# Input units of the first half written whole: fifteen high products, sixteen low products, the closing high one

## The chip, the cores and the metric

One core of a Trainium2 chip runs the whole program. The metric is the device time of one execution in microseconds (us); the time before is the median of three runs. TensorE (PE) multiplies, ScalarE (ACT) and VectorE (DVE) work on tiles in SBUF and PSUM, GpSimd is POOL, and SyncE (SP) issues nearly all loads of weights.

## The reference

One layer of a hybrid encoder trunk on x of 256 tokens by 2048 features, in float32:

```python
u = rms_norm(x); proj = u @ w_in            # 2048 x 12,580 columns
y_a = stick_breaking_attention(...)         # 4 heads x 128
y_b = forgetting_attention(...)             # 4 heads x 128
y_c = rwkv7_time_mix(...)                   # 16 heads x 64, a recurrence over 256 tokens
m = sum_i sigmoid(gate_i) * (y_i @ P_i)
x = x + rms_norm(m @ w_out)
x = x + rms_norm(relu(rms_norm(x) @ w_up)**2 @ w_down)
```

What matters here is `proj`: a product of the transposed input (2048 rows, that is sixteen blocks of 128) with blocks of 128 columns of `w_in`.

## The kernel before

**Split products.** Every matrix is used as the sum of two float32r parts. The input `u` is split into sixteen tiles `pk`, each of 128 x 512: the high part of the 256 tokens in the left half, the low part in the right half. A weight half tile of 128 x 1024 (eight blocks of 128 x 128, 512 KB) is loaded by SP into a buffer `raw`; ACT copies it to `whi`, the high part (L158), and DVE subtracts that from `raw` into `wlo`, the low part (L159). A *high product* multiplies a block of `whi` with all 512 columns of a `pk` tile, a *low product* a block of `wlo` with the left 256 columns alone. Sixteen of each make one *input unit*, a PSUM tile `gps` of 128 x 512, whose two halves are added when it is read.

**Units.** `unit` makes one input unit out of two half tiles. `gemm` writes eight high and eight low products of a half tile; in the second half the last high product comes last of all (L182), since it writes all 512 columns and closes the sum. Lines: L174 high, L178 low, L182 closing. `unit` is called 39 times, all in the first 320 us: for five of the eight query and key tiles of the stick-breaking attention (h = 3 to 7, at 24 to 54 us; the first three are written by hand), for eight of the forgetting attention, two low-rank ones and 24 of the RWKV branch. The other users of `gemm`, the up-projection of the MLP, do not go through `unit`. Between groups of units `tok` makes token-major products, in which each product, high or low, has 512 columns (L204, L220).

**Buffers and order.** `raw`, `whi` and `wlo` have three buffers each, in turn. `wnext` hands out the next split half tile and sees that one more is already asked for (`AHEAD = 1`). A `wlo` buffer comes free when its last low product is done, a `raw` buffer when its `wlo` has been written; SP issues loads in order, so a load waits for the DVE split that frees its buffer. PE runs in the order in which the program writes its instructions. ACT and DVE are put in order by a scheduler when the program is built, and then run strictly in that order.

**Beside the units.** The attention and RWKV steps are generators. `tick`, called after every two high or four low products, moves a clock and lets the generators write their next instructions between the products. At h = 4 `norm` works out 1/rms of the tokens (`rstd`: ACT L247 and L248, DVE L249 to L252); `scaled` (L403) multiplies the finished tiles by it. At h = 7 `narrow_weights` (L418) builds a small weight tile out of two further `raw` loads.

Of the kernel before, what the change touches and what calls it, by code (L numbers as in the profile page):

```python
# [17 lines left out]
T = 256  # L18
D = 2048
KT = 16  # L20
AHEAD = 1
SETTLE = 2.6
US = 0.227
# [27 lines left out]
def hybrid_block(ctx, tc, xt, x, gains, params, consts, lora, gup, wst, out):  # L51
    nc = tc.nc
    V, A, G, PE = nc.vector, nc.scalar, nc.gpsimd, nc.tensor
# [15 lines left out]
    def gps():  # L69
        return pg.tile([128, 512], F32, tag="gps", name=nm("gps"), bufs=4)  # L70
# [35 lines left out]
    def step(th):  # L106

        if th["need"] is not None:
            if th["need"] not in at or clock[0] < at[th["need"]] + SETTLE:
                return False  # L110
            th["need"] = None
        if clock[0] < th["due"]:
            return False
        try:
            r = next(th["gen"])
        except StopIteration:
            threads.remove(th)
            return True
        if isinstance(r, str):
            th["need"] = r  # L120
        else:
            th["due"] = clock[0] + r
        return True

    def tick(us):

        clock[0] += us
        while any([step(th) for th in list(threads)]):
            pass
# [13 lines left out]
    def wraw(n=None):  # L143
        raw = wpool.tile([128, HALF], F32, tag="raw", name=nm("raw"), bufs=3)
        nc.sync.dma_start(out=raw, in_=wst[wpos[0] if n is None else n])
        wpos[0] = (wpos[0] if n is None else n) + 1
        return raw
# [3 lines left out]
    def wsplit(raw):  # L151
        home = homes.pop(0) if homes else None
        if home:
            hi, lo = home(), home()
        else:
            hi = wpool.tile([128, HALF], F32R, tag="whi", name=nm("whi"), bufs=3)
            lo = wpool.tile([128, HALF], F32R, tag="wlo", name=nm("wlo"), bufs=3)
        A.activation(hi, raw, AF.Copy)  # L158
        V.tensor_tensor(lo, raw, hi.bitcast(F32), ALU.subtract)  # L159
        wq.append((hi, lo))  # L160

    def wnext():

        while len(wq) < 1 + AHEAD and (order or wpos[0] < wst.shape[0]):
            wsplit(wraw(order.pop(0) if order else None))
            if side:
                side.pop(0)()
        return wq.pop(0)

    def gemm(ps, hi, lo, pks, first, last, tick=lambda us: None):  # L170

        n = len(pks)
        for i in range(n - 1 if last else n):
            PE.matmul(ps, hi[:, i * 128:i * 128 + 128], pks[i], start=first and i == 0, stop=False)  # L174
            if i % 2:
                tick(2 * US)
        for i in range(n):
            PE.matmul(ps[:, 0:T], lo[:, i * 128:i * 128 + 128], pks[i][:, 0:T], start=False, stop=False)  # L178
            if i % 4 == 3:
                tick(2 * US)  # L180
        if last:
            PE.matmul(ps, hi[:, (n - 1) * 128:n * 128], pks[n - 1], start=False, stop=True)  # L182

    def unit(pks):

        ps = gps()
        for h in range(2):
            hi, lo = wnext()
            gemm(ps, hi, lo, pks[8 * h:8 * h + 8], h == 0, h == 1, tick)
        return ps  # L190

    def tok(pks, lag=1):
# [253 lines left out]
    for h in range(8):  # L446
        if h == 7:
            wz = narrow_weights()
        ps = qb[h] if h < 3 else unit(upk)
        qk.append(g1())  # L450
        evac(ps, qk[h])
        if h == 4:
            ms = norm()
        if h == 6:
            turned_rstd(ms)
        for i in range(h + 1) if h == 4 else [h] if h > 4 else []:
            scaled(qk[i])
# [621 lines left out]
    def low_rank(i):  # L1079
        nme, n = (("zx", 128), ("zy", 128))[i]  # L1080
        ps = unit(upk)
        z = rp.tile([128, T], F32, tag=nme, name=nme, bufs=1)
        shift(ps, MU_X + i, z[0:n], n)
        done[nme] = z
# [3 lines left out]
    for s in ("q", "k"):  # L1088
        lst = []
        for h in range(4):  # L1090
            ps = unit(upk)
            t = g1()
            evac(ps, t)
            scaled(t)
            lst.append(t)
        done["fox" + s] = lst
# [7 lines left out]
    for hf in range(2):  # L1104
        for s, mo in (("k", MU_K), ("r", MU_R), ("v", MU_V)):
            for p in range(4 * hf, 4 * hf + 4):
                ps = unit(upk)
# [213 lines left out]
    work, urgent, tasks, hl = [], [], [], {}  # L1321
# [237 lines left out]
    for j in range(2):  # L1559
        up(j)  # L1560
        ps, post = heads[j]
# [241 lines left out]
```

## Time and profile before

| | us |
|---|---|
| median of three runs | 1492.98 (1491.58 to 1494.12) |
| the profiled execution's own time | 1491.24 |
| its span, first to last instruction | 1489.5 |
| PE busy | 1476.4 (99%) |
| DVE busy | 1214.5 (82%) |
| ACT busy | 933.4 (63%) |
| granted clock of PE, mean | 0.998 |

The table gives each engine's busy time within the span. PE's is nearly the span; the other engines work beside it. Names such as `whi<-raw` say which tile is written from which.

### The profile page before, as it was taken

What the parts mean: (1) busy time and instruction counts of PE and PEld (TensorE: products, weight loads), DVE (VectorE), ACT (ScalarE), POOL (GpSimd) and SP (SyncE); (2) the same over time, 40 slices, a digit from 0 to 9 for tenths busy, and PEclk for the clock granted to TensorE, in tenths of its full rate; (3) what the DMA queues carried; (4) which work ended last, traced back from release to release, by engine and by line L of the source; (5) the groups of instructions that cost most, each with busy time, mean ns of one, the idle gap of its engine ahead of it and who ended that gap; (6) DMA issues with size and microseconds to landing.
All of it is one profiled execution on the core that took longest, in us unless ns stands there. A gap on an engine that the chain in (4) does not pass through costs nothing.

```text
span 1489.5 us, 22848 instructions
## 1 busy us (share of the span) xinstructions
PE 1476.4 (99%) x8427; PEld 1248.4 (84%) x8427; DVE 1214.5 (82%) x1688; ACT 933.4 (63%) x1394; POOL 90.0 (6%) x160
## 2 busy tenths in 40 slices
PE   9999999999999999999999999999999999999997
PEld 8888888888778888788888888888888888888885
DVE  7676778999678898567647788999899999999986
ACT  7465666654576554474444777776767767777653
POOL 0011000100001100000000000000000000000000
PEclk9999999999999999999999999999999999999999
DMA  7545454545544546445855768888888887989874
GB/s 285 189 164 183 161 177 169 184 159 198 174 148 167 183 164 208 142 158 189 272 193 207 273 209 254 255 257 255 247 255 251 267 256 223 260 249 283 259 249 155
DMA packets 107759, 317.70 MB, mean 213 GB/s; under 512 B 10752, under 2 KB 14976, under 8 KB 107392
## 3 DMA queue, kind: packets, MB, share of 16 engines
q1 hardware_dynamic: 94688, 284.39, 55.4%
q0 software_dynamic: 8064, 29.36, 10.6%
q10 hardware_dynamic: 4896, 2.49, 0.6%
q8 instruction: 66, 1.08, 0.3%
q14 instruction: 45, 0.37, 0.1%
HBM read 282.65 MB, written 4.19 MB: 193 GB/s over the span
## 4 chain that ended last, share of the span: by engine, by line
PE 98%; DVE 1%; DMA 0%; issue 0%; ACT 0%; POOLq 0%; POOL 0%; DVEq 0%; ACTq 0%
PE gps L220 28%; PE gps L174 23%; PE gps L178 13%; PE gps L204 7%; PE mps L1511 3%; PE mps L1512 3%; PE mps L1513 3%; PE gps L1511 3%; PE gps L1513 3%; PE gps L1512 3%; PE gps L182 2%; PE gps L340 1%; PE mps L828 1%; PE gps L1270 0%; PE gps L338 0%; DMA x<-in_xt_dram 0%
## 5 line engine op out<-in xcount | busy, mean ns | idle before, releaser
L159 DVE TENSOR_TENSOR wlo<-raw,whi 128x1024 fp32r<-128x1024 f32 x495 | 600.9, 1221 | 154.2 <-ACT whi L158 139.4
L158 ACT ACTIVATE whi<-raw 128x1024 fp32r<-128x1024 f32 x495 | 521.5, 1057 | 253.9 <-PE gps L220 87.4
L174 PE MATMUL gps<-pk,whi 128*128 128x512 f32 x1321 | 332.4, 392 | 0.0
L220 PE MATMUL gps<-whi,pk 128*128 128x512 f32 x1136 | 286.4, 392 | 0.0
L174 PEld LDWEIGHTS gps<-pk,whi 128*128 128x128 f32 x1321 | 244.7, 188 | 47.6
L220 PEld LDWEIGHTS gps<-whi,pk 128*128 128x128 f32 x1136 | 211.4, 188 | 44.1 <-issue 0.4
L178 PEld LDWEIGHTS gps<-pk,wlo 128*128 128x128 f32 x1408 | 192.0, 190 | 13.6
L178 PE MATMUL gps<-pk,wlo 128*128 128x256 f32 x1408 | 196.9, 283 | 0.0
L220 PE MATMUL gps<-wlo,pk 128*128 128x512 f32 x568 | 155.3, 392 | 0.0
L220 PEld LDWEIGHTS gps<-wlo,pk 128*128 128x128 f32 x568 | 105.7, 188 | 22.0
L1374 DVE TENSOR_TENSOR sp<-raw,sp 128x1024 fp32r<-128x1024 f32 x67 | 81.7, 1220 | 3.4 <-ACT sp L1373 3.1
L1402 ACT ACTIVATE sp<-gps 128x512 f32<-128x512 f32 x52 | 31.1, 598 | 84.3 <-PE gps L182 84.3
L1373 ACT ACTIVATE sp<-raw 128x1024 fp32r<-128x1024 f32 x67 | 70.7, 1055 | 14.1 <-PE mps L1512 5.1
L204 PE MATMUL gps<-whi,pk 128*128 128x512 f32 x256 | 68.9, 390 | 0.0
L1511 PE MATMUL mps<-whi,fm 128*128 128x512 f32 x168 | 66.2, 394 | 0.0
L1512 PE MATMUL mps<-whi,fm 128*128 128x512 f32 x168 | 65.8, 392 | 0.0
L1513 PE MATMUL mps<-wlo,fm 128*128 128x512 f32 x168 | 65.6, 390 | 0.0
L1473 POOL DMA_DIRECT2D raw<-raw x40 | 35.0, 874 | 427.4 <-DVE raw L1470 108.4
L204 PEld LDWEIGHTS gps<-whi,pk 128*128 128x128 f32 x256 | 47.8, 188 | 9.9
L1511 PE MATMUL gps<-whi,fm 128*128 128x512 f32 x126 | 49.3, 391 | 0.0
L1513 PE MATMUL gps<-wlo,fm 128*128 128x512 f32 x126 | 49.1, 390 | 0.0
L1470 DVE TENSOR_TENSOR raw<-raw,raw 128x1024 f32<-128x1024 f32 x40 | 48.8, 1220 | 0.4
(400 smaller groups left out, 2013.4 us busy)
## 6 DMA issues: line engine op xcount, KB each, us to landing
raw<-in_wst_dram SPq DMA_DIRECT2D x499, 512.0 KB, 4.4
raw<-raw POOLq DMA_DIRECT2D x40, 512.0 KB, 6.4
sp<-in_wst_dram SPq DMA_DIRECT2D x16, 512.0 KB, 5.3
raw<-sp POOLq DMA_DIRECT2D x8, 512.0 KB, 6.2
sp<-raw POOLq DMA_DIRECT2D x8, 512.0 KB, 6.4
x<-in_x_dram SPq DMA_DIRECT2D x8, 256.0 KB, 5.5
xs<-x SPq DMA_DIRECT2D x2, 1024.0 KB, 4.8
x<-xs SPq DMA_DIRECT2D x4, 512.0 KB, 6.5
```

Of the source, the lines that this page charges most:

```text
L158: A.activation(hi, raw, AF.Copy)
L159: V.tensor_tensor(lo, raw, hi.bitcast(F32), ALU.subtract)
L174: PE.matmul(ps, hi[:, i * 128:i * 128 + 128], pks[i], start=first and i == 0, stop=False)
L178: PE.matmul(ps[:, 0:T], lo[:, i * 128:i * 128 + 128], pks[i][:, 0:T], start=False, stop=False)
L204: PE.matmul(ps[tt], pks[k][:, c:c + 128], w[:, (k - k0) * 512:(k - k0) * 512 + 512], start=k == 0 and part == 0 and w is hl[0], stop=w is ...
L220: PE.matmul(ps[tt], pks[k][:, c:c + 128], w[:, (k - k0) * 512:(k - k0) * 512 + 512], start=k == 0 and part == 0 and w is hl[0], stop=False)
L1373: A.activation(hi, raw, AF.Copy)
L1374: V.tensor_tensor(lo, raw, hi.bitcast(F32), ALU.subtract)
L1470: V.tensor_tensor(x, x, z, ALU.add)
L1511: PE.matmul(Q[f], p, w, start=d == 0 and i == 0, stop=False)
L1512: PE.matmul(Q[f], pl, w, start=False, stop=False)
L1513: PE.matmul(Q[f], p, wl, start=False, stop=d == nd - 1 and i == 1)
```

## The change

`unit` no longer calls `gemm`. It writes fifteen high products through both half tiles, then sixteen low products through both, then the sixteenth high product. The second `wnext` now stands between the eighth and the ninth high product. The calls of `tick` are as many as before (eleven in a unit), seven among the high and four among the low products.

```diff
     def unit(pks):
 
         ps = gps()
-        for h in range(2):
-            hi, lo = wnext()
-            gemm(ps, hi, lo, pks[8 * h:8 * h + 8], h == 0, h == 1, tick)
+        hl = []
+
+        def high(k):
+            PE.matmul(ps, hl[k // 8][0][:, k % 8 * 128:k % 8 * 128 + 128], pks[k], start=k == 0, stop=k == KT - 1)
+
+        for k in range(KT - 1):
+            if k % 8 == 0:
+                hl.append(wnext())
+            high(k)
+            if k % 2:
+                tick(2 * US)
+        for k in range(KT):
+            PE.matmul(ps[:, 0:T], hl[k // 8][1][:, k % 8 * 128:k % 8 * 128 + 128], pks[k][:, 0:T], start=False, stop=False)
+            if k % 4 == 3:
+                tick(2 * US)
+        high(KT - 1)
         return ps
```

Lines below the change stand 13 further down in the changed kernel (L249 becomes L262, L403 L416); high products are now L190, low ones L199. Numbers at the end of names are running numbers and differ a little between the programs: `whi_539` of before is `whi_531` now.

PE, the middle of the unit h = 7, before: the end of the first half's high products, its low products, and the start of the second half's.

```order
L174 MATMUL gps_577<-pk_190,whi_539 128x512
L174 MATMUL gps_577<-pk_193,whi_539 128x512
L178 MATMUL gps_577<-pk_132,wlo_540 128x256
L178 MATMUL gps_577<-pk_135,wlo_540 128x256
L178 MATMUL gps_577<-pk_144,wlo_540 128x256
L178 MATMUL gps_577<-pk_147,wlo_540 128x256
L178 MATMUL gps_577<-pk_180,wlo_540 128x256
L178 MATMUL gps_577<-pk_183,wlo_540 128x256
L178 MATMUL gps_577<-pk_190,wlo_540 128x256
L178 MATMUL gps_577<-pk_193,wlo_540 128x256
L174 MATMUL gps_577<-pk_222,whi_580 128x512
L174 MATMUL gps_577<-pk_225,whi_580 128x512
```

The same place now:

```order
L190 MATMUL gps_577<-pk_190,whi_531 128x512
L190 MATMUL gps_577<-pk_193,whi_531 128x512
L190 MATMUL gps_577<-pk_222,whi_580 128x512
L190 MATMUL gps_577<-pk_225,whi_580 128x512
L190 MATMUL gps_577<-pk_228,whi_580 128x512
L190 MATMUL gps_577<-pk_231,whi_580 128x512
L190 MATMUL gps_577<-pk_244,whi_580 128x512
L190 MATMUL gps_577<-pk_247,whi_580 128x512
L190 MATMUL gps_577<-pk_250,whi_580 128x512
L199 MATMUL gps_577<-pk_132,wlo_532 128x256
L199 MATMUL gps_577<-pk_135,wlo_532 128x256
L199 MATMUL gps_577<-pk_144,wlo_532 128x256
```

The first use of `whi_580`, the second half's high part, moved forward past the eight low products of the first half.

DVE, at the end of h = 5, before: splits of weights (L159) and the steps of 1/rms (L249 to L252).

```order
L159 TENSOR_TENSOR wlo_490<-raw_487,whi_489 128x1024
L159 TENSOR_TENSOR wlo_518<-raw_515,whi_517 128x1024
L249 TENSOR_TENSOR tmp_451<-rstd_312 128x256
L250 TENSOR_TENSOR tmp_451<-tmp_451,tmp_450 128x256
L251 TENSOR_SCALAR tmp_451<-tmp_451 128x256
L252 TENSOR_TENSOR rstd_312<-rstd_312,tmp_451 128x256
L234 TENSOR_TENSOR g_76_509<-gps_464,tmp_510 128x256
L403 TENSOR_TENSOR g_45_343<-g_45_343,rstd_312 128x256
```

The same place now:

```order
L159 TENSOR_TENSOR wlo_482<-raw_479,whi_481 128x1024
L262 TENSOR_TENSOR tmp_451<-rstd_312 128x256
L263 TENSOR_TENSOR tmp_451<-tmp_451,tmp_450 128x256
L159 TENSOR_TENSOR wlo_518<-raw_515,whi_517 128x1024
L264 TENSOR_SCALAR tmp_451<-tmp_451 128x256
L265 TENSOR_TENSOR rstd_312<-rstd_312,tmp_451 128x256
L247 TENSOR_TENSOR g_76_509<-gps_464,tmp_510 128x256
L416 TENSOR_TENSOR g_45_343<-g_45_343,rstd_312 128x256
```

The split `wlo_518` (second half of h = 6) moved back past two steps of 1/rms. In both programs five more rows of `scaled` follow, then the split of the first half of h = 7 (`wlo_540`, now `wlo_532`) and the two rows of `narrow_weights`.

## Rows read from the trace of the kernel before

**Rows 1.** The page: span and busy time by engine.
```profile
span 1489.5 us, 22848 instructions
...
PE 1476.4 (99%) x8427; PEld 1248.4 (84%) x8427; DVE 1214.5 (82%) x1688; ACT 933.4 (63%) x1394; POOL 90.0 (6%) x160
```

**Rows 2.** Waits of PE, whole span: total us, times, longest.
```profile
PE mps L281 <- DVE zt L278: 1.2, 1, 1.2
PE gps L340 <- DVE pk L243: 0.9, 1, 0.9
PE mps L1255 <- DVE x L1217: 0.5, 1, 0.5
PE mps L962 <- DVE XT L949: 0.3, 1, 0.3
```

**Rows 3.** Timeline of PE, one unit: start, us, line, operation, shape, count.
```profile
104.58 2.00 PE L174 MATMUL gps<-pk,whi 128*128 128x512 f32 x8
106.41 1.11 PE L178 MATMUL gps<-pk,wlo 128*128 128x256 f32 x8
107.36 1.78 PE L174 MATMUL gps<-pk,whi 128*128 128x512 f32 x7
108.97 1.12 PE L178 MATMUL gps<-pk,wlo 128*128 128x256 f32 x8
...
110.16 2.00 PE L174 MATMUL gps<-pk,whi 128*128 128x512 f32 x8
```

**Rows 4.** Timeline of PE in a stretch of 512-column products alone.
```profile
68.76 1.97 PE L220 MATMUL gps<-whi,pk 128*128 128x512 f32 x8
...
71.48 1.98 PE L220 MATMUL gps<-whi,pk 128*128 128x512 f32 x8
```

**Rows 5.** Timeline of PE, the unit h = 7.
```profile
48.32 2.12 PE L174 MATMUL gps<-pk,whi 128*128 128x512 f32 x8
50.28 1.11 PE L178 MATMUL gps<-pk,wlo 128*128 128x256 f32 x8
51.23 1.78 PE L174 MATMUL gps<-pk,whi 128*128 128x512 f32 x7
```

**Rows 6.** Timeline of ACT, 36 to 52 us: two of its rows.
```profile
41.19 0.42 ACT L248 ACTIVATE rstd<-tmp 128x256 f32<-128x256 f32 x1
...
50.00 1.06 ACT L158 ACTIVATE whi<-raw 128x1024 fp32r<-128x1024 f32 x1 [1.72 <-DMA raw<-in_wst_dram]
```

**Rows 7.** Timeline of SP's queue: the load for the second half of h = 7.
```profile
46.82 0.33 SPq L145 DMA_DIRECT2D raw<-in_wst_dram  x1
```

**Rows 8.** Timeline of DVE, 39 to 47 us.
```profile
39.91 1.22 DVE L159 TENSOR_TENSOR wlo<-raw,whi 128x1024 fp32r<-128x1024 f32 x1 [1.47 <-ACT whi L158]
41.64 0.42 DVE L249 TENSOR_TENSOR tmp<-rstd 128x256 f32<-128x256 f32 x1 [0.51 <-ACT rstd L248]
42.10 0.43 DVE L250 TENSOR_TENSOR tmp<-tmp,tmp 128x256 f32<-128x256 f32 x1
...
45.57 1.22 DVE L159 TENSOR_TENSOR wlo<-raw,whi 128x1024 fp32r<-128x1024 f32 x1
46.71 1.29 DVE L418 TENSOR_TENSOR wz<-raw,par 128x512 f32<-128x512 f32 x2
```

**Rows 9.** Loads of L145 from 40 to 50 us (four).
```profile
DMA to landing us min/median/max: 3.1/4.8/6.7
```

**Rows 10.** Timeline of ACT: the split of the second half used at 107.36.
```profile
103.87 1.05 ACT L158 ACTIVATE whi<-raw 128x1024 fp32r<-128x1024 f32 x1
```

**Rows 11.** Timeline of DVE, 244 to 264 us: the split used at 262.33.
```profile
260.80 1.21 DVE L159 TENSOR_TENSOR wlo<-raw,whi 128x1024 fp32r<-128x1024 f32 x1
```

**Rows 12.** Timeline of PE, 255 to 266 us.
```profile
256.74 1.12 PE L178 MATMUL gps<-pk,wlo 128*128 128x256 f32 x8
...
262.33 0.63 PE L178 MATMUL gps<-pk,wlo 128*128 128x256 f32 x4
```

**Rows 13.** Stage of 0 to 10 us: busy by engine, granted clock, DMA.
```profile
0.00:10.00 10.00, 7.96 (x26) 6.17 (x27) 4.90 (x13) 5.98 (x12) 2.18 (x15) 1.00 0.82 270
```

## The prediction, made before the changed kernel ran

> **What bounds the kernel now.** I read the page's head first: in a span of 1489.5 us PE is busy for 1476.4, 99% [rows 1]. So a change pays only where PE's own stream gets shorter, and costs wherever PE is made to wait. Next the view of waits for PE: over the whole span it names four, of 1.2, 0.9, 0.5 and 0.3 us, and none of them in the 39 units, so there is no stall in them to take away [rows 2]. Third, the timeline of PE in a unit that nothing interrupts: 8 high products, 8 low, 7 high, 8 low and the closing one, 5.58 us from one unit's start to the next (104.58 to 110.16) [rows 3]. Fourth, unit by unit, the ACT and DVE timelines against PE's: how long before its first product each split is ready. That slack is what the new order spends.
>
> **What it adds and removes on PE.** The products are the same ones; only the number of changes between kinds falls, from two of each sort in a unit to one. What does a change cost? Where all products have 512 columns, twelve (eight high, then four low ones that the row left out holds) take 2.72 us (68.76 to 71.48), 0.227 each [rows 4]; eight low ones take 0.95 (106.41 to 107.36), 0.119 each [rows 3]. Sixteen high at 0.227 and sixteen low at 0.119 make 3.63 + 1.90 = 5.53 us, and the unit takes 5.58: 0.05 for its two alternations. One of them goes: 0.025 a unit, 1.0 us over 39. With 0.120 for a low one (8 in 0.96) it is 0.015 and 0.6 us. I take 0.7 us of gain; 0 and 1.0 are its ends.
>
> **What it moves: the second half's high part.** It is wanted after 8 high products rather than after 8 high and 8 low, 0.95 us earlier. A second half whose split was ready by more than that stays hidden. I read all 39. The shortest slack after h = 7 is 2.44 us: split from 103.87 to 104.92, first product at 107.36 [rows 10, 3]; 1.5 us would be left. One fails, in h = 7. There `narrow_weights` takes two `raw` buffers out of turn, so the load of the second half cannot be issued until 46.82, when the DVE split that started at 45.57 ended and freed its buffer [rows 7, 8]; ACT gets the data at 50.00 and ends the split at 51.06 [rows 6]. The product is at 51.23, a slack of 0.17 [rows 5]. In the new order PE arrives when its eight high products are done, at 50.28: it would wait 51.06 - 50.28 = 0.78 us.
>
> **What else moves there: a split on DVE.** `wlo_518` (second half of h = 6) ran at 39.91, in time in which DVE had nothing to do until 1/rms came from ACT at 41.61 (41.19 + 0.42) [rows 6, 8]. The buffer it is to write is now read by low products that come seven high products later, and the scheduler has put it behind two steps of 1/rms. DVE runs in order, so the rest of 1/rms, six rows of `scaled` and the split that frees the buffer wait for it. Its price is the step from one such split to the next instruction, 45.57 to 46.71, 1.14 us [rows 8]. The freeing split then starts at 46.71, the load is issued at 47.96, and with the same 3.18 us from issue to ACT (46.82 to 50.00) and 1.06 of split it is ready at 52.20. PE waits 52.20 - 50.28 = 1.92 us. The order is not a guess: it is fixed when the program is built. What the trace doesn't show is how long that load will take beside its neighbours. The four loads of 40 to 50 us landed after 3.1 to 6.7 us [rows 9]: with 6.7 instead of 3.1 the wait is 5.5 us; with no delay on DVE it is 0.78. I take 1.9, the row of this very load, as the burst behind it (two more loads freed by `narrow_weights`) only moves with it.
>
> **What it moves: low parts.** The first half's low products start seven high products later, so its `wlo` buffer comes free 1.6 us later (107.36 to 108.97) [rows 3], in every unit. The split that reuses it belongs to the second half of the next unit, whose low products start when they did before, 15 high and 8 low products into the unit. Nearly everywhere its slack is longer than 1.6 us, and where it is not, DVE is late because of other work and not for the buffer. The tightest: the split from 260.80 to 262.01, for a product at 262.33 [rows 11, 12], a slack of 0.32. Its buffer is last read by low products of a first half that now end, at the latest, about when the second half's began before, 256.74 [rows 12] (seven high products later than they did); that is 4 us before the split starts. The scheduler also puts this one behind the same steps as before, less two short ones that move ahead. I cost it at nothing; if that cover fails, it is the first rival. The attention steps get their DVE work sooner, since what now waits is the split behind them, and the ticks fall within 0.2 us of where they did. SP's loads follow the splits by up to 1.6 us, but a load is issued three half tiles ahead of its use, some 8 us (three times half of 5.58), and lands in 3.1 to 6.7 [rows 3, 9]: nothing, but for h = 7.
>
> **The sum.** -0.7 + 1.9 = +1.2 us. Profiled execution: span 1489.5, own time 1491.24, which becomes 1492.4. The median of the runs shown is 1.74 above that, 1492.98, and becomes **1494.2 us**. A measurement of this kernel can tell about 0.2%, 3.0 us, from no change: the forecast is "no difference that can be told", with its sign towards slower.
>
> **Rivals.**
> *Late low splits (slower).* The RWKV steps come in four heads' pairs, of which the place at 262 us is the first, and DVE has hardly a gap there. If the 1.6 us by which the buffer comes later is passed on whole, and the slack is as short in each, PE waits 1.6 - 0.32 = 1.3 us four times, 5.1 us: 1499.3. It decides from the point at which the split ends more than 0.32 us later than now. For it: the slack of 0.32. Against it: 4 us between the buffer's release and the split.
> *The stall lowers the clock (slower).* An idle PE of 1.9 us might lose its full clock; all products that are left of that unit, 0.95 + 2.9 us, would take twice as long, and perhaps the 5.6 us behind them: +3.8 to +9.4, about 1500 with 5.6. It decides from the length of the pause. The only pause among products here, 0.9 us before L340, left the granted clock at 1.00 (2.4 GHz) in its stage [rows 2, 13]; twice that length is not shown.
> The Trainium skill, "TensorE: Matmul & The Clock Gate", section "Why this matters for your kernels", says that idle gaps between bursts of matmuls put the clock back to half. The trace neither bears it out nor excludes it for a gap of this length.
> *The stall does not come (no difference).* The load lands so much sooner that ACT is ready at 50.28. Then the junctions are all: -0.7, 1492.3. For it: h = 7 lies near the start, where small shifts add up. Against it: 3.1 us is the shortest landing of the group [rows 9].
> *Long runs go faster (faster).* A low product has half the columns of a high one; if in a long run it took half of 0.227 us, 0.1135 for 0.119, a unit would gain 16 x 0.0055 = 0.09 us and the kernel 3.4: 1490.8 with the stall, 1488.9 without it. For it: what the low ones spend beyond half may belong to the change of kind. Against it: 0.95 and 0.96 us for eight after seven or eight high ones show no such share [rows 3].
>
> **How the numbers follow.** Forecast 0.74; late low splits 0.08; clock 0.05; no stall 0.08; faster runs 0.03, two thirds of it without the stall; something else 0.02, shared by both sides. Of the forecast's 0.74 I give 0.03 to the long landing (+4.8 us, slower by more than 0.2%). Faster by over 0.2%: 0.02 + 0.01 = 0.03. Slower: 0.08 + 0.05 + 0.03 + 0.01 = 0.17, of which I take 0.02 back for rivals that come only in part: 0.15. Within 0.2%: 0.82. The range reaches from the case without a stall and the larger gain (1492.0), less half a microsecond for the spread of the runs, to most of the long landing: 1491.5 to 1497.5; the two slower rivals lie beyond it.
>
> **What will show it.** Right: one new wait of PE in the unit h = 7, before its ninth high product at about 50.3 us, of 1.9 us, ended by ACT's `whi`; SP's load at about 47.96 instead of 46.82; undisturbed units of 5.55 to 5.57 us; no wait in the other 38. Wrong: PE waits for `wlo` at the RWKV steps from 262 us on, a second new wait for `whi`, or a granted clock under 1.00 after 50 us.

## The result, and the profile after

| | before | after |
|---|---|---|
| median (us) | 1492.86 (1491.58 to 1494.12, 22 runs) | 1494.95 (1493.36 to 1500.72, 22 runs) |
| ratio after / before | | 1.0016 [1.0011, 1.0022] |
| the profiled execution's own time | 1491.24 | 1495.62 |
| its span | 1489.5 | 1493.8 |

The change costs 2.1 us by the medians; the interval of the ratio, times 1492.9, allows 1.6 to 3.3. The forecast was +1.2, 1494.2 us. The sign is the forecast one, and the interval lies clear of 1; by the forecast's bound of 0.2% the ratio is no difference, with the interval's upper end just beyond it.

The page of after, busy time by engine, as [rows 1]:

```profile
PE 1477.9 (99%) x8427; PEld 1248.4 (84%) x8427; DVE 1215.6 (81%) x1688; ACT 932.6 (62%) x1394; POOL 94.3 (6%) x160
```

As many products as before. That PE is busy for 1.5 us longer is no sign of the change: the control below, in the old order, has 1477.9 too. The view of waits of PE over the span, which answers to [rows 2] (total us, times, longest):

```profile
PE gps L190 <- ACT whi L158: 1.8, 1, 1.8
PE mps L294 <- DVE zt L291: 1.2, 1, 1.2
PE gps L174 <- DVE junk L1531: 1.0, 1, 1.0
PE gps L1526 <- DVE wlo L159: 0.9, 2, 0.5
...
```

L294 and two left out, of 0.5 and 0.3 us, are waits of before, 13 lines down; before's 0.9 us at L340 isn't there. One wait belongs to the units: a high product (L190) that waits once for a split on ACT, 1.8 us. No line says L199: no low product has a wait that the view lists (its shortest lines here are of 0.2 us). L174 and L1526 are new too, but lie in the MLP after 1200 us; the last two experiments are about them.

PE's timeline around the new wait, to hold against [rows 5] (start, length, operation, and in brackets the idle time before it and what ended it):

```profile
47.97 2.11 PE L190 MATMUL gps<-pk,whi 128*128 128x512 f32 x8
51.91 1.89 PE L190 MATMUL gps<-pk,whi 128*128 128x512 f32 x7 [1.84 <-ACT whi L158]
53.64 2.08 PE L199 MATMUL gps<-pk,wlo 128*128 128x256 f32 x16
55.55 0.39 PE L190 MATMUL gps<-pk,whi 128*128 128x512 f32 x1
```

This is the unit h = 7, and the wait stands before its ninth high product. Back along the chain: ACT's split, SP's load (the first of three in its line) and DVE, as [rows 6 to 8]:

```profile
50.81 1.06 ACT L158 ACTIVATE whi<-raw 128x1024 fp32r<-128x1024 f32 x1 [2.88 <-DMA raw<-in_wst_dram]
```

```profile
47.51 1.53 SPq L145 DMA_DIRECT2D raw<-in_wst_dram  x3
```

```profile
41.32 0.43 DVE L262 TENSOR_TENSOR tmp<-rstd 128x256 f32<-128x256 f32 x1 [3.20 <-ACT rstd L261]
41.78 0.42 DVE L263 TENSOR_TENSOR tmp<-tmp,tmp 128x256 f32<-128x256 f32 x1
42.12 1.22 DVE L159 TENSOR_TENSOR wlo<-raw,whi 128x1024 fp32r<-128x1024 f32 x1
43.26 0.29 DVE L264 TENSOR_SCALAR tmp<-tmp 128x256 f32<-128x256 f32 x1
...
46.27 1.22 DVE L159 TENSOR_TENSOR wlo<-raw,whi 128x1024 fp32r<-128x1024 f32 x1
47.40 1.28 DVE L431 TENSOR_TENSOR wz<-raw,par 128x512 f32<-128x512 f32 x2
```

DVE is idle for 3.20 us while it waits for 1/rms, and only then, between two steps of it, does the split that it used to do in that time. The split that frees the `raw` buffer starts at 46.27 and the load is issued at 47.51. This execution reaches h = 7 0.35 us sooner than that of before (47.97 for 48.32; the wait at L340, at 7 to 8 us, is the one that it doesn't have), so on the clock of [rows 7] the load is issued at 47.86 rather than 46.82: 1.04 us later.

An undisturbed stretch of PE, as [rows 3] (sixteen high products in a row are the closing one of a unit and fifteen of the next):

```profile
100.47 3.82 PE L190 MATMUL gps<-pk,whi 128*128 128x512 f32 x16
104.12 2.08 PE L199 MATMUL gps<-pk,wlo 128*128 128x256 f32 x16
106.04 3.82 PE L190 MATMUL gps<-pk,whi 128*128 128x512 f32 x16
...
111.60 3.82 PE L190 MATMUL gps<-pk,whi 128*128 128x512 f32 x16
```

A unit takes 5.57 and 5.56 us, before 5.58. The first half in two windows (busy time of PE, PEld, DVE, ACT and POOL, then the granted clock, DMA share and GB/s):

```profile
48.00:60.00 12.00, 10.16 (x67) 7.49 (x67) 6.12 (x11) 3.85 (x6) 1.65 (x1) 1.00 0.66 227
60.00:326.00 266.00, 266.00 (x1579) 232.09 (x1581) 201.93 (x318) 166.84 (x263) 26.55 (x60) 1.00 0.52 175
```

PE is idle for 1.84 us in the first and for nothing in the second, and the granted clock is 1.00 (2.4 GHz) in both.

Two points of PE's stream serve as marks from here on: the closing product of h = 7 (0.39 us, at 53 to 57 us), and the first group of 64x128 products of the RWKV steps after the last unit (1.16 us). Between them stand the 34 units behind h = 7. First the kernel before, then the one after:

```profile
53.80 0.39 PE L182 MATMUL gps<-pk,whi 128*128 128x512 f32 x1
...
318.63 1.16 PE L828 MATMUL mps<-Bt,At 64*128 64x128 f32 x16
```

```profile
319.95 1.16 PE L841 MATMUL mps<-Bt,At 64*128 64x128 f32 x16
```

From 53.80 to 318.63 it is 264.83 us before, and from 55.55 (above) to 319.95 it is 264.40 now: 34 whole units give 0.43 us, 0.013 each. The unit h = 7, from its first product to its closing one, takes 5.48 us before (48.32 to 53.80) and 7.58 now (47.97 to 55.55): +2.10. So at the second mark the kernel has lost 2.10 - 0.43 = 1.67 us, nearly the whole difference of the medians. The profiled execution ends 4.3 us after that of before (spans 1493.8 and 1489.5). At the second mark it is only 1.32 later (1.67 less the 0.35 by which it came sooner); the other 3.0 us lie behind the units, in stages that the change doesn't touch.

### The profile page after: what moved, and what is told of

It is laid out like the page before. It is cut to its first block, busy times and chain, and to the rows that moved or that the text cites. A ratio compares the mean times of both kernels' runs of the same rounds, so it can differ in the third digit from the quotient of the medians.

```text
span 1493.8 us, 22855 instructions
## 1 busy us (share of the span) xinstructions
PE 1477.9 (99%) x8427; PEld 1248.4 (84%) x8427; DVE 1215.6 (81%) x1688; ACT 932.6 (62%) x1394; POOL 94.3 (6%) x160
## 4 chain that ended last, share of the span: by engine, by line
PE 97%; DVE 2%; issue 1%; ACT 0%; DMA 0%; POOLq 0%; POOL 0%; DVEq 0%; ACTq 0%
PE gps L233 28%; PE gps L174 14%; PE gps L190 9%; PE gps L178 8%; PE gps L217 7%; PE gps L199 5%; PE mps L1524 3%; PE mps L1525 3%; PE mps L1526 3%; PE gps L1526 2%; PE gps L1524 2%; PE gps L1525 2%; PE gps L182 1%; PE gps L353 1%; DVE wlo L159 1%
## 5 line engine op out<-in xcount | busy, mean ns | idle before, releaser
L159 DVE TENSOR_TENSOR wlo<-raw,whi 128x1024 fp32r<-128x1024 f32 x495 | 602.0, 1223 | 156.2 <-ACT whi L158 128.1
L233 PEld LDWEIGHTS gps<-whi,pk 128*128 128x128 f32 x1136 | 211.3, 188 | 44.3 <-issue 0.4
L174 PE MATMUL gps<-pk,whi 128*128 128x512 f32 x736 | 183.5, 390 | 1.0 <-DVE junk L1531 1.0
L174 PEld LDWEIGHTS gps<-pk,whi 128*128 128x128 f32 x736 | 137.4, 188 | 29.4 <-ACT pk L1425 1.4
L190 PE MATMUL gps<-pk,whi 128*128 128x512 f32 x624 | 153.0, 393 | 1.8 <-ACT whi L158 1.8
L190 PEld LDWEIGHTS gps<-pk,whi 128*128 128x128 f32 x624 | 114.3, 188 | 24.1 <-ACT whi L158 2.3
L178 PEld LDWEIGHTS gps<-pk,wlo 128*128 128x128 f32 x784 | 106.9, 190 | 7.5
L178 PE MATMUL gps<-pk,wlo 128*128 128x256 f32 x784 | 109.3, 282 | 0.0
L199 PEld LDWEIGHTS gps<-pk,wlo 128*128 128x128 f32 x624 | 80.3, 191 | 3.1
L199 PE MATMUL gps<-pk,wlo 128*128 128x256 f32 x624 | 81.8, 283 | 0.0
L1526 PE MATMUL mps<-wlo,fm 128*128 128x512 f32 x168 | 65.5, 390 | 0.0
```

The costliest lines, as they stand in the source:

```text
L190: PE.matmul(ps, hl[k // 8][0][:, k % 8 * 128:k % 8 * 128 + 128], pks[k], start=k == 0, stop=k == KT - 1)
L199: PE.matmul(ps[:, 0:T], hl[k // 8][1][:, k % 8 * 128:k % 8 * 128 + 128], pks[k][:, 0:T], start=False, stop=False)
L233: PE.matmul(ps[tt], pks[k][:, c:c + 128], w[:, (k - k0) * 512:(k - k0) * 512 + 512], start=k == 0 and part == 0 and w is hl[0], stop=False)
L1526: PE.matmul(Q[f], p, wl, start=False, stop=d == nd - 1 and i == 1)
```

## The experiments

The theory (A in the expectations) is the forecast's: whole units gain a little each, and lose one stall in h = 7, made of an earlier use of the second half's high part and of a late load behind a moved split on DVE. The rivals ask whether another part of the units loses too, and (E) whether a late start of all that follows costs more than the delay itself, through new waits in the MLP. The first four ran together on one chip (before: 1493.16 us, 33 runs), the last four on another (before: 1493.28 us, 33 runs).

**The two loads of `narrow_weights` in buffers of their own** (an edit of the kernel after). The loads of h = 7 then wait for nothing that `narrow_weights` holds.

```diff
-            V.tensor_tensor(wz[:, ks], wraw(28 + h).rearrange("p (k c) -> p k c", k=8)[:, :, 0:64],
+            raw = rp.tile([128, HALF], F32, tag="m", name=nm("raw"), bufs=4)
+            nc.sync.dma_start(out=raw, in_=wst[28 + h])
+            V.tensor_tensor(wz[:, ks], raw.rearrange("p (k c) -> p k c", k=8)[:, :, 0:64],
```

> The changed kernel, but the two loads of narrow_weights go to buffers of their own, so the load for the second half of h = 7 no longer waits for the DVE split that frees a raw buffer. Theory A (the loss is the one wait of PE in h = 7, 1.84 us in the profile of the changed kernel, less 0.4 to 0.7 us that the junctions give back): no wait of PE in h = 7; about 1492.4 us, 2.5 less than the changed kernel's 1494.95 and at or a little under before's 1492.86. Rival B (part of the loss arises late in the kernel, where the profile of the changed kernel shows new waits of 1.0 and 0.9 us in the MLP): the wait in h = 7 goes, but some 1 us stays, 1493.3 to 1493.8 us, and the MLP's waits are there again.

Measured: 1492.01 us (1491.4 to 1493.43, 11 runs), ratio to before 0.9993 [0.9984, 1.0002]. PE's timeline in h = 7 and at the second mark:

```profile
48.49 3.70 PE L190 MATMUL gps<-pk,whi 128*128 128x512 f32 x15
...
53.94 0.39 PE L190 MATMUL gps<-pk,whi 128*128 128x512 f32 x1
...
318.35 1.16 PE L843 MATMUL mps<-Bt,At 64*128 64x128 f32 x16
```

Fifteen high products run on without a break; the unit takes 5.45 us, and the 34 behind it again 264.41, 0.42 us less than before. DVE does the moved split where the changed kernel does it (42.64, between two steps of 1/rms), but the load no longer waits for what comes after. The whole stall is gone, so it hung on that load alone, and there are no waits in the MLP (rival B had 1 us of them stay). The median is the lowest of all kernels, but its interval holds 1: a gain over before isn't shown.

**The moved split back in its place** (of after). The low part of the second half of h = 6 gets a buffer of its own (`homes` lists, split by split, where the parts go), so DVE does it ahead of 1/rms again; the use of the second half stays as early as the change made it.

```diff
+    def apart():
+        calls.append(0)
+        if len(calls) == 1:
+            return wpool.tile([128, HALF], F32R, tag="whi", name=nm("whi"), bufs=3)
+        return rp.tile([128, HALF], F32R, tag="m", name=nm("wlo"), bufs=4)
+
+    homes[:] = [None] * 7 + [apart]
```

> The changed kernel, but the low part of the second half of h = 6 has a buffer of its own, so the scheduler puts that split ahead of 1/rms on DVE again, as in the kernel before. Theory A (of the 1.84 us, about 1.05 is the split that stands in the way on DVE and 0.78 the earlier use alone): PE waits 0.7 to 0.9 us in h = 7, and the time is about 1.05 us under the changed kernel, 1493.9. Rival C (the load is late for another reason, the order of 1/rms on DVE doesn't matter): the wait stays at 1.8 us and the time at 1494.9.

Measured: 1493.8 us (1491.89 to 1496.3, 11 runs), ratio 1.0006 [0.9997, 1.0015]. Its timelines of PE, SP and ACT in h = 7:

```profile
48.16 2.11 PE L190 MATMUL gps<-pk,whi 128*128 128x512 f32 x8
51.46 1.88 PE L190 MATMUL gps<-pk,whi 128*128 128x512 f32 x7 [1.19 <-ACT whi L158]
```

```profile
46.69 1.53 SPq L145 DMA_DIRECT2D raw<-in_wst_dram  x3
```

```profile
50.35 1.06 ACT L158 ACTIVATE whi<-raw 128x1024 fp32r<-128x1024 f32 x1 [2.23 <-DMA raw<-in_wst_dram]
```

DVE does the split at 39.78, ahead of 1/rms again. The load is issued at 46.69, against h = 7's start only 0.03 us later than before (1.47 before it, before 1.50), so the term on DVE is gone. The wait is 1.19, outside the expected 0.7 to 0.9, since the data took 3.66 us from issue to ACT (46.69 to 50.35), where [rows 6, 7] have 3.18. The moved split's term is borne out (rival C, another cause of the late load, had the wait stay at 1.8); how long the load takes from execution to execution decides several tenths of what is left.

**The unit h = 7 in halves, the other 38 whole** (of after; `halves` is the old text of `unit`, `whole` the new one). Here the earlier use is undone, and the moved split stays.

```diff
-        ps = qb[h] if h < 3 else unit(upk)
+        ps = qb[h] if h < 3 else (halves if h == 7 else whole)(upk)
```

> The changed kernel, but the unit h = 7 alone is written in two half units as before; the other 38 stay whole. Theory A: PE comes to the second half 0.95 us later, so of 1.84 us some 0.9 is left (0.8 to 1.0), in front of the ninth high product; about 1494.0 us. Rival D (the earlier use costs little by itself, each of the 38 others costs something): the time stays within 0.3 us of the changed kernel, 1494.7 or more.

Measured: 1493.91 us (1492.38 to 1494.97, 11 runs), ratio 1.0006 [0.9997, 1.0015]. PE in h = 7:

```profile
50.45 1.11 PE L178 MATMUL gps<-pk,wlo 128*128 128x256 f32 x8
52.44 1.89 PE L174 MATMUL gps<-pk,whi 128*128 128x512 f32 x7 [0.87 <-ACT whi L158]
```

The eight low products cover part of the wait, and 0.87 us is left: the late load alone makes PE wait even in the old order. The times of this kernel and the last one can't be told from before's, nor clearly from the changed kernel's; that each takes away a part of the stall is read from the profiles.

**Only h = 5, 6 and 7 whole** (of before). If the loss is theirs, three units must cost what all 39 do, and a little more, as the other units no longer gain.

```diff
-        ps = qb[h] if h < 3 else unit(upk)
+        ps = qb[h] if h < 3 else (whole if h > 4 else halves)(upk)
```

> The kernel before, but the units h = 5, 6 and 7 alone are written whole; the other 36 in half units. Theory A: the wait is there in full, 1.7 to 1.9 us, and only three of 39 junctions are gone; the time is 1.8 us over before, about 1494.6 us. Rival D (the loss is spread over the units): three of 39 units carry a thirteenth of it, 1493.0 us, and no wait over 0.3 us in h = 7.

Measured: 1495.26 us (1493.53 to 1498.48, 11 runs), ratio 1.0018 [1.001, 1.0027]. PE in h = 7 and at the second mark:

```profile
48.24 2.11 PE L198 MATMUL gps<-pk,whi 128*128 128x512 f32 x8
52.44 1.88 PE L198 MATMUL gps<-pk,whi 128*128 128x512 f32 x7 [2.08 <-ACT whi L158]
...
56.08 0.39 PE L198 MATMUL gps<-pk,whi 128*128 128x512 f32 x1
...
320.91 1.16 PE L851 MATMUL mps<-Bt,At 64*128 64x128 f32 x16
```

The loss is there whole (rival D, a loss spread over the units, had 1493.0 us): h = 7 takes 7.84 us, 2.36 more than before, and the wait is a little over the expected 1.7 to 1.9. The stretch behind it, all in halves, takes 264.83 us, exactly as before; in all seven profiles in which it is whole it takes 264.40 or 264.41. So the 0.43 us of the changed kernel comes from its units.

**The control: the loads apart in the kernel before** (the edit of the first experiment, put into before).

> Control: the kernel before, in half units, with the two loads of narrow_weights in buffers of their own. Before has no wait in h = 7, so theory A expects nothing from them: 1492.9 to 1493.2 us, within 0.5 of before, and no wait of PE in the units; against the whole units with the same buffers (1492.01) it should be some 0.5 us slower, by the junctions. Rival: the separate buffers help by themselves, and this one is at 1492.0 as well, so that whole units give nothing.

Measured: 1493.09 us (1491.13 to 1495.32, 11 runs), ratio 0.9999 [0.999, 1.0008]. The buffers alone give nothing that can be told, so what the first experiment took away was the changed kernel's stall and not a cost of before. Against the first experiment, which ran on the other chip, the control is slower as expected, but the intervals of the two ratios overlap; the gain of whole units shows at the marks alone. There the stretch behind h = 7 takes 265.01 us, 0.18 more than the other two in halves, and all of the 0.18 arises at the place of the slack of 0.32 us [rows 11, 12]: DVE's split starts at 261.17 for 260.80, ends at 262.38, and the low products that want it start at 262.44. The seven high products before them take 1.69 us to that start, before 1.62, and the first four low ones 0.67 for 0.56. So in the old order that slack is used up in one execution and not in another.

The control shows one thing more, in the waits of PE, in a kernel without a stall in h = 7:

```profile
PE gps L1515 <- DVE wlo L159: 0.5, 1, 0.5
...
PE gps L174 <- DVE junk L1520: 0.2, 1, 0.2
```

These are the MLP's waits, at the places of after's L1526 and L174 (the MLP's lines stand 11 further up here).

**A delay of 2 us, and of 4 us, without any stall** (of the first experiment's kernel). Nine extra high products, or eighteen (`range(18)` and `i == 17`), whose sum is not read, stand in front of h = 7. If a late start costs more than itself (E), these show it.

```diff
+        if h == 7:
+            burn = mps()
+            for i in range(9):
+                PE.matmul(burn, upk[0][:, 0:128], upk[1], start=i == 0, stop=i == 8)
```

> Whole units with separate buffers (1492.01 us, no wait), plus nine extra high products in front of h = 7 that write a tile nobody reads: everything behind is 9 x 0.227 = 2.0 us later, with no stall. Theory A (a delay in the first half costs its own length): 1494.05 us. Rival E (whatever comes about 2 us later makes loads in the MLP land late, as in the profiles of the changed kernel and of two variants, PE then waits there for low splits, 0.9 to 1.0 us): 1495.0 us, with such waits in the profile.

> As the last one with eighteen extra products, 4.1 us. Theory A: 1496.1 us. Rival E: 1497.0 us or more, with waits of PE for low splits in the MLP. If these waits come and go from profile to profile without regard to the delay, they are chance.

Measured: with nine 1494.91 us (1492.96 to 1496.73, 11 runs), ratio 1.0008 [0.9999, 1.0017]; with eighteen 1496.49 (1495.33 to 1498.91, 11 runs), ratio 1.0022 [1.0013, 1.0031]. The median of nine lies at E's value, that of eighteen between the two (A 1496.1, E 1497.0 or more), so the times decide nothing; by the ratios to before, each taken on its own chip, the delays cost 0.0015 and 0.0029 of the time, 2.2 and 4.3 us for products of 2.0 and 4.1, but the intervals are wide enough for E too. Two of the waits with nine, in the MLP, then all waits with eighteen:

```profile
PE mps L1532 <- DVE sp L1393: 0.5, 1, 0.5
PE gps L1532 <- DVE wlo L159: 0.5, 1, 0.5
```

```profile
PE mps L294 <- DVE zt L291: 1.2, 1, 1.2
PE gps L353 <- DVE pk L256: 0.6, 1, 0.6
PE mps L1274 <- DVE x L1236: 0.5, 1, 0.5
PE mps L981 <- DVE XT L968: 0.3, 1, 0.3
```

With nine E's waits are there, 1.0 us together; with eighteen all four waits are at before's places (13 to 19 lines down), although the delay is twice that of the changed kernel. The control has such waits without any delay. So the waits don't follow the delay, which speaks against E. Up to the second mark a delay is passed on as it is: from the first product at h = 7, extra ones included, to that mark it is 271.89 us with nine and 273.93 with eighteen, where the first experiment has 269.86: 2.03 and 4.07 more.

**The changed kernel again.**

> The changed kernel once more. Theory A: 1494.95 us within 0.6, the wait of 1.8 us in h = 7 again; the MLP's waits of 1.0 and 0.9 us may be absent (chance) or there again (rival E).

Measured: 1495.08 us (1492.95 to 1496.93, 11 runs), ratio 1.0011 [1.0002, 1.0019]. All waits of PE in its profile, then the load, the split, and PE in h = 7 and at the second mark:

```profile
PE gps L190 <- ACT whi L158: 2.1, 1, 2.1
PE mps L294 <- DVE zt L291: 1.2, 1, 1.2
PE mps L1268 <- DVE x L1230: 0.5, 1, 0.5
PE gps L353 <- DVE pk L256: 0.4, 1, 0.4
PE mps L975 <- DVE XT L962: 0.3, 1, 0.3
PE mps L1177 <- DVE m L1152: 0.2, 1, 0.2
```

```profile
47.90 1.53 SPq L145 DMA_DIRECT2D raw<-in_wst_dram  x3
```

```profile
51.47 1.06 ACT L158 ACTIVATE whi<-raw 128x1024 fp32r<-128x1024 f32 x1 [3.15 <-DMA raw<-in_wst_dram]
```

```profile
48.36 2.11 PE L190 MATMUL gps<-pk,whi 128*128 128x512 f32 x8
52.58 1.89 PE L190 MATMUL gps<-pk,whi 128*128 128x512 f32 x7 [2.10 <-ACT whi L158]
...
56.21 0.39 PE L190 MATMUL gps<-pk,whi 128*128 128x512 f32 x1
...
320.62 1.16 PE L841 MATMUL mps<-Bt,At 64*128 64x128 f32 x16
```

The stall is back, with 2.10 us, and the MLP's two waits are not. Over the profiles those come and go, up to 1.9 us together, with the change (the first profile) and without (the control): they are taken as scatter of single executions, not its effect. From the second mark to the end of the span before took 1170.9 us, the first experiment's kernel 1171.3, eighteen 1171.2, the changed kernel 1173.9 and then 1172.0, nine 1173.2 and the control, without whole units, 1173.1: a spread of 3.0 us that follows neither the change nor the delay. Single profiles can't exclude that the change adds a few tenths there on average. The units behind h = 7 take 264.41 us, within 0.01 of the two profiles above that have them whole; h = 7 takes 7.85, +2.37. The load needs 3.57 us from issue to ACT (47.90 to 51.47), 0.27 more than in the first profile, and the wait is 0.26 longer.

## Why the prediction was right

**The new wait, its place and its cause: right.** One wait, in h = 7, before the ninth high product, ended by ACT's `whi`; none in the other 38 units. The two terms are told apart on the chip: without the earlier use 0.87 us is left, without the moved split 1.19, with the `narrow_weights` loads out of the way nothing.

**The size of the wait: nearly right.** In starts, as the forecast had it: eight high products take 1.96 us to the next product (48.32 to 50.28 [rows 5]), so PE is due at 49.93 in the first profile of after and goes on at 51.91, 1.98 late; in the second 50.32 and 52.58, 2.26 late; with three units whole 50.20 and 52.44, 2.24. Forecast: 1.92. Its term on DVE came out at 1.04 for 1.14 (in the second profile too: issued at 47.90, with h = 7 at 48.36 for 48.32). Its load, taken over from [rows 6, 7] with 3.18 us, took 3.30 (47.51 to 50.81) in the first and 3.57 in the second: the one row that the forecast had is the shortest of all that the runs gave. That 1.92 comes so near to the first profile's 1.98 is in part luck, one term 0.10 too long and the other 0.12 too short. And a cost was left out: the seven products after the pause take 1.73 us (51.91 to 53.64) where seven such take 1.61 without one (107.36 to 108.97 [rows 3]), 0.12 more. So h = 7 lost 2.10 to 2.37. (The view puts the wait at 1.84 and not 1.98 because it counts from the end of the eighth product, which the profile models: 50.07, that is 51.91 - 1.84, 0.14 after the ninth was due; in an unbroken run the next product starts before the last has ended.)

**The gain at the alternations: there, but mis-sized.** 0.013 us a unit over 34 of them, 0.5 carried over to 39, where the sum has 0.7. The ends, 0 and 1.0, hold it; the smaller of the two readings (0.120 for a low product) was the better one.

**The sum.** With both terms as measured it is 2.10 to 2.37 less 0.5: +1.6 to +1.9, for +1.2. The forecast was short on both sides: 0.2 to 0.5 us too little stall, 0.2 too much gain. The medians say +2.1 [1.6, 3.3], and +1.8 [0.3, 2.8] when the changed kernel ran again. What is left, 0.2 to 0.5, is no more than the interval; whether it is anything stays open.

**What was costed at nothing: right.** The low parts, whose buffers come free later, make no product of the first half of the kernel wait, at 262 us or elsewhere. The later buffers do show on DVE: between 20 and 326 us its splits wait three times, 5.0 us in all, for low products (L199) to free a `wlo` buffer (four times and 7.8 us in the second profile), where the view of before lists no such wait. They still end early enough for PE. At 262 us the slack even grew: in the first profile of after the split ends at 261.62 and its products come at about 263.7 (262.76 and eight low ones of 0.119), 2.1 us later, where before had 0.32. So the rival of the late low splits falls: it would have been four waits of 1.3 us for `wlo` before 326 us, and PE has none there.

**The clock: the rival falls.** A pause of 1.84 us left the granted clock at 1.00 in the window around it and in the one behind, and one of 2.10 us (the changed kernel again) did too; the seven products right behind it took 1.73 us, not twice 1.61. The rule of the Trainium skill, "TensorE: Matmul & The Clock Gate", section "Why this matters for your kernels", that idle gaps between bursts bring the half clock back, did not come to bear on a gap of this length; what a longer one does here no run shows.

**The other two.** That the stall would not come is refuted by both profiles of the changed kernel. That long runs of low products go faster is refuted by 16 of them in 1.92 us (104.12 to 106.04): 0.120 each, no less than in runs of eight.

**A better version.** Whole units with the loads apart are the only form run here that keeps the gain without the stall. Their 1492.01 us (ratio 0.9993 [0.9984, 1.0002]) beat the changed kernel, and can't be told from the one before.

## What to carry to other kernels

Before products are grouped by kind, list for each operand the slack between its readiness and its new first use, and for each buffer its new last use: here one slack of 0.17 us out of 39 decided the sign, and a gain of 0.013 us a unit had to pay for it. Then compare the built order on the other engines too, for a scheduler may answer a buffer that comes free later by moving work into the chain that feeds the very operand that is now wanted sooner. A single profile that is 4 us longer is not yet a loss of 4 us: compare positions at fixed marks of the bounding engine's stream, and the waits of several executions.

## What the runs showed of the hardware beyond that

After a pause of 1.84 us the first seven 512-column products took 0.12 us longer than the same seven with no pause before them, at a granted clock of 1.00. A pause isn't needed for that: the eight at the start of h = 7, right behind four small products of four columns (L395), take 1.96 us before (48.32 to 50.28 [rows 5]), where eight between low ones take 1.83 (104.58 to 106.41 [rows 3]). The same load of 512 KB, for the second half of h = 7, reached ACT after 3.18 us (before), 3.30 and 3.57 (the changed kernel twice), 3.30 (h = 7 in halves), 3.55 (three units whole) and 3.66 (the moved split back in its place). And waits of PE in the MLP, up to 1.9 us in all, appear in one execution of a kernel and not in the next, and the part of the span behind the units, 1170.9 to 1173.9 us, varied by 3.0 us over the profiles.
